# An encoder layer in hi/lo splits: where loads, conversions and the embedding's gate stand in the engines' orders

## The chip, the core and the metric

The kernel runs on one core of a Trainium2 chip. The core has a matrix engine (TensorE, PE in the profile), a vector engine (VectorE, DVE), an engine for activation functions (ScalarE, ACT), a general engine (GpSimd, POOL) and SyncE (SP), which here only issues transfers. Each of them runs its own instructions in order; among each other they are held together by semaphores. Transfers are issued on the queues of SP, ACT and POOL and carried by 16 shared DMA engines. The metric is the device time of one launch, in microseconds. Before the change it was 1231.56 us, the median of three runs (1228.37 to 1232.48).

## The reference

One post-norm encoder layer over 1024 tokens of width 1024, all in float32. Half of the mixer's heads do bidirectional retention, the other half windowed attention; then comes a SwiGLU feed-forward part, and beside it an embedding per layer that a gate lets through.

```python
u = jnp.einsum('bsd,de->bse', h, w_in[i])
rq, rk, rv, rg, aq, ak, av = jnp.split(u, split_points, axis=-1)
y_ret = _bidirectional_retention(rq, rk, rv, lg_f, lg_b, ret_gn_gain[i], rg)   # group norm, times silu(rg)
y_att = _windowed_gqa(aq, ak, av, attn_sink[i])                                # +-128 tokens, ALiBi, sinks
mix = jnp.einsum('bse,ed->bsd', jnp.concatenate([y_ret, y_att], axis=-1), w_out[i])
h = _layer_norm(ALPHA * h + mix, ln1_gain[i], ln1_bias[i])
g = jnp.einsum('bsd,df->bsf', h, w_ffn_gate[i])
up = jnp.einsum('bsd,df->bsf', h, w_ffn_up[i])
ffn = jnp.einsum('bsf,fd->bsd', jax.nn.silu(g) * up, w_ffn_down[i])
ple = jnp.einsum('bsr,rd->bsd', p[i], w_ple_proj[i])
ple_gate = jax.nn.sigmoid(jnp.einsum('bsd,de->bse', h, w_ple_gate[i]))
h = _layer_norm(ALPHA * h + ffn + ple_gate * ple, ln2_gain[i], ln2_bias[i])
```

## The kernel before

Every dense product is made in three matmuls (`mm3`, L82). Each operand is first cut into a high part in the fast matmul type and the rest (`split`, L78): ScalarE copies with rounding (L79), VectorE subtracts (L80). Most dense products also use a seven-product scheme for 2x2 blocks in place of eight, so sums of weight blocks and of activation blocks are made first (POOL and VectorE), and the seven results are added and subtracted behind (VectorE).

The program has five stages, in us of the profiled execution:

- **First products and dense projections**, 0 to about 150. Five pairs of projections, each in seven products. `seq1` (L296) is the order of the products, `x_put(c)` cuts the last sums of activations, `pahead(n)` (L303) cuts the weights of the next products.
- **Mixers**, about 150 to 405, in four head pairs, numbered 0 to 3, with boundaries near 210, 275 and 340. Per pair the retention and the attention are short matmuls with much work of the other engines between. To fill TensorE, a queue of dense work is interleaved: ten tiles of 16 steps (`mtile`, `spill`, `gate`, `embedding`; `enqueue`, L474), 36 steps per pair, taken where the list of `run` (L828 on, built in the loop over the pairs) has an F. Loads and cuts of a tile are hung on the first steps of the tile ahead of it. `load_pair` (L513) loads the next pair's keys, queries and the attention's raw queries, and `conv_q` (L314) converts these for two groups g (ScalarE scales, L323; VectorE takes the rest, L324). `rv_load` and `turned` (L489 to L509) load the retention's values and transpose them on TensorE (L495). `norm` and `scale` are the group norm: VectorE sums, ScalarE squares, POOL takes a power (`sm`, L634), VectorE multiplies (L635). `wsum` (L435) builds sums of the gate's weights in DRAM with POOL transfers (L444 to L448).
- **Output projection and first layer norm**, to 505.
- **Gate products** `ple` (L1058), 505 to 582: h @ w_ple_gate in seven products (`prod`, L1011). Each finished gate tile (128x1024) goes through a sigmoid on ScalarE; `fetch` brings the embedding's product back from DRAM (`ed`), `embed_next` multiplies on VectorE (L1052) and adds to the accumulator `zd` in DRAM by an accumulating transfer (L1053), both transfers on POOL's queue.
- **FFN**: gate and up in 11 weight pairs of 14 products each (`gunits`, 582 to about 1012), down (to 1200), second layer norm (to 1232.6). `Pair.load` brings the weights, `s_sums` makes sums of them on POOL (L1133 to L1139), `prep` cuts, `post` evacuates (L1180, L1186).

What sets the order: in the mixers TensorE and POOL run in the order of the source (`manual_schedule`), while ScalarE, VectorE and SP are ordered by a scheduler at build time. From `ple` on, all engines run in the order of the source. Buffers come from pools; tiles of one tag share a few slots, and a new tile's first writer waits for the old tile's last reader. The tag `raw` (`rawt`, L97) has two slots: raw weights, raw queries and raw values go through them in the mixers.

## Time and profile before

| | us |
|---|---|
| median of three runs | 1231.56 |
| the profiled execution, whole | 1234.39 |
| its span from first to last instruction | 1232.6 |
| TensorE busy | 1201.4 |
| TensorE busy in 150 to 405 (255 us, mixers) | 245.90 |
| TensorE busy in 582 to 1012 (430 us, FFN gate and up) | 421.13 |
| TensorE busy in 1200 to 1232 (32 us, the end) | 23.63 |

The mean granted clock of TensorE was 0.993. A row of a timeline has the start in us, the busy time, the engine, the line of the source, the operation, and out<-in by the names of the program; in square brackets stands the idle time of the engine just before and what ended it. SPq, ACTq and POOLq rows are issues of transfers. A row of the waits names the engine and line that waited, the engine, tile and line it waited for, then the total, the count and the longest. In the rows of windows, PEclk is the clock that TensorE was granted in the stretch, 1.00 being full.

### The profile page before, as it was taken

The numbers are of one execution on the slowest core, as the hardware profiler recorded it, in microseconds if no ns is written. First come the engines' busy times: TensorE is split into PE (matmuls) and PEld (weight loads), VectorE is DVE, ScalarE is ACT, GpSimd is POOL, SyncE is SP. The second block draws the span as 40 slices with busy tenths as digits, with TensorE's granted clock in tenths as the row PEclk, the third lists the DMA queues.
The fourth block names the chain that finished last, engine by engine and source line by source line (L and its number), as shares of the span: only waits on it lengthen the run. The fifth ranks groups of instructions, "written<-read, shape, count | busy, mean of one in ns | idle before, by whom it ended". The sixth has DMA issues, their size and how long they took to land.

```text
span 1232.6 us, 16444 instructions
## 1 busy us (share of the span) xinstructions
PE 1201.4 (97%) x5911; PEld 988.4 (80%) x5911; DVE 760.1 (62%) x1258; ACT 522.8 (42%) x968; POOL 455.7 (37%) x395
## 2 busy tenths in 40 slices
PE   9999999989999999999899999999999999999997
PEld 7778877878887888887688888888888888888885
DVE  6954665666665548884665454555445555875678
ACT  4532555666675502462333223333323334652432
POOL 1651113120111002332477556466564523024235
PEclk9999999999999999999899999999999999999999
DMA  6222445572300432358631233321333149999987
GB/s 222 90 87 103 145 137 150 164 225 92 114 18 18 140 117 96 131 166 241 143 140 74 73 126 128 128 77 69 112 128 128 69 137 281 372 273 209 263 197 204
DMA packets 69521, 178.43 MB, mean 145 GB/s; under 512 B 8128, under 2 KB 10304, under 8 KB 69440
## 3 DMA queue, kind: packets, MB, share of 16 engines
q1 hardware_dynamic: 54016, 139.64, 32.3%
q0 software_dynamic: 14848, 35.66, 14.4%
q10 hardware_dynamic: 576, 2.10, 0.4%
q8 instruction: 46, 0.75, 0.2%
q14 instruction: 35, 0.29, 0.1%
HBM read 124.67 MB, written 47.45 MB: 140 GB/s over the span
## 4 chain that ended last, share of the span: by engine, by line
PE 65%; DMA 13%; DVE 8%; issue 7%; POOL 4%; ACT 3%; ACTq 0%; SPq 0%; DVEq 0%; POOLq 0%
PE bs L287 4%; PE bs L289 4%; PE bs L288 4%; PE bt L287 3%; PE bo L287 3%; PE bt L288 3%; PE bt L289 3%; PE bo L289 3%; PE bo L288 3%; PE bmm L287 3%; PE bmm L288 3%; PE bmm L289 3%; PE bmm L83 3%; PE bmm L85 3%; PE bmm L84 3%
## 5 line engine op out<-in xcount | busy, mean ns | idle before, releaser
L1165 POOL TENSOR_TENSOR ev<-ev 128x512 f32<-128x512 f32 x33 | 54.9, 1663 | 91.0 <-DVE ev L1180 62.2
L80 DVE TENSOR_TENSOR w<-H,w 128x512 fp32r<-128x512 f32 x44 | 42.2, 959 | 65.1 <-ACT w L79 65.1
L80 DVE TENSOR_TENSOR w<-raw,w 128x512 fp32r<-128x512 f32 x55 | 45.8, 841 | 44.9 <-ACT w L79 44.8
L1163 ACT ACTIVATE ev<-ev 128x512 f32<-128x512 f32 x33 | 20.9, 632 | 102.0 <-DVE ev L1180 102.0
L1169 POOL TENSOR_TENSOR ev<-ev,ev 128x512 f32<-128x512 f32 x44 | 62.7, 1436 | 2.6
L83 PE MATMUL bmm<-H,w 128*128 128x512 f32 x144 | 61.3, 426 | 0.3 <-ACT H L79 0.3
L80 DVE TENSOR_TENSOR u<-H,u 128x512 fp32r<-128x512 f32 x47 | 35.5, 755 | 39.4 <-ACT u L79 39.1
L1133 POOL TENSOR_TENSOR H<-ln 128x512 f32<-128x512 f32 x22 | 29.0, 1318 | 81.2 <-DMA ln<-in_w_gu 75.3
L84 PE MATMUL bmm<-H,w 128*128 128x512 f32 x144 | 57.0, 396 | 0.0
L85 PE MATMUL bmm<-H,w 128*128 128x512 f32 x144 | 56.9, 395 | 0.0
L666 POOL COPY sc<-skb 128x2 f32<-128x2 f32 x32 | 6.2, 202 | 135.3 <-PE bt L686 87.6
L852 POOL TENSOR_TENSOR stt<-stt,cst 128x1 f32<-128x1 f32 x8 | 11.5, 1451 | 99.7 <-DVE stt L851 99.7
L79 ACT ACTIVATE u<-H 128x512 fp32r<-128x512 f32 x47 | 29.6, 630 | 40.8 <-PE bmm L289 9.0
L674 ACT ACTIVATE sc<-sc,st 128x385 f32<-128x385 f32 (+1 forms) x64 | 37.3, 584 | 15.9 <-DVE st L671 15.8
L79 ACT ACTIVATE w<-raw 128x512 fp32r<-128x512 f32 x55 | 33.6, 622 | 23.1 <-PE bt L289 6.7
L80 DVE TENSOR_TENSOR u<-raw,u 128x512 fp32r<-128x512 f32 x32 | 36.5, 1146 | 5.8 <-ACT u L79 5.8
L678 ACT ACTIVATE sc<-sc,st 128x384 f32<-128x384 f32 (+1 forms) x64 | 34.1, 580 | 10.4 <-DVE st L676 10.4
L79 ACT ACTIVATE w<-H 128x512 fp32r<-128x512 f32 x44 | 27.4, 622 | 24.4 <-PE bs L289 6.3
L1139 POOL TENSOR_TENSOR H<-H,raw 128x512 f32<-128x512 f32 x22 | 36.8, 1697 | 0.0
L1135 POOL TENSOR_TENSOR H<-H,raw 128x512 f32<-128x512 f32 x22 | 35.0, 1592 | 1.7
L671 DVE CUSTOM_DVE_ANT_0 sc<-cst,bs,skb 128x384 f32<-128x384 f32 (+1 forms) x64 | 35.0, 575 | 0.7 <-PE bs L670 0.4
L83 PEld LDWEIGHTS bmm<-H,w 128*128 128x128 f32 x144 | 27.4, 190 | 6.6 <-issue 1.6
(886 smaller groups left out, 4036.3 us busy)
## 6 DMA issues: line engine op xcount, KB each, us to landing
ad<-ev SPq DMA_DIRECT2D x33, 512.0 KB, 2.6
raw<-in_w_gu SPq DMA_DIRECT2D x22, 512.0 KB, 4.4
ln<-in_w_gu SPq DMA_DIRECT2D x22, 512.0 KB, 3.5
raw<-ad SPq DMA_DIRECT2D x40, 256.0 KB, 5.9
ln<-ad SPq DMA_DIRECT2D x37, 256.0 KB, 6.4
H<-in_w_dn SPq DMA_DIRECT2D x33, 256.0 KB, 7.9
raw<-in_w_mt SPq DMA_DIRECT2D x14, 512.0 KB, 3.6
A<-in_w_pg POOLq DMA_DIRECT2D x12, 512.0 KB, 5.5
```

Of the source, the lines that this page charges most:

```text
L79: act.activation(hi, raw, AF.Copy)
L80: dve.tensor_tensor(lo, raw, hi.bitcast(F32), ALU.subtract)
L83: pe.matmul(o, lh, rh, start=start, stop=False)
L84: pe.matmul(o, lh, rl, start=False, stop=False)
L85: pe.matmul(o, ll, rh, start=False, stop=stop)
L287: pe.matmul(o, lh, rh, start=start, stop=False, skip_group_check=True)
L288: pe.matmul(o, lh, rl, start=False, stop=False, skip_group_check=True)
L289: pe.matmul(o, ll, rh, start=False, stop=stop, skip_group_check=True)
L674: act.activation(sc[:, g, :nk + 1], sc[:, g, :nk + 1], AF.Exp, bias=st_[:, 0, j, g:g + 1], scale=-1.0, accum_out=st_[:, 2, j, g:g + 1])
L1139: pool.tensor_tensor(s[3], s[0], a(0, 1), ALU.subtract)
L1165: pool.tensor_tensor(c[:, 1, :], c[:, 0, :], c[:, 1, :], ALU.mult)
L1169: pool.tensor_tensor(self.ev[dst][:, 0, :], left, right, op)
```

## The change

1. **Dense products.** `pahead(4)` moves ahead of `x_put(3)`, so weights of the first products are cut ahead of the last sums of activations. Product 2 of projection 1 moves from fourth place to between products 7 and 4 of projection 0; in the last projection 2 and 7 change places, and with them the two halves of the attention's queries.
2. **Mixers.** SP, too, now runs in the order of the source. A tile's load stands at step 0 of the tile ahead of it, its two cuts at steps 6 and 9 (step 12 for the embedding's first rows). The cuts are tied on ScalarE behind the activation that the source has just ahead (`in_order`). `load_pair` only loads; the two halves of `conv_q` come later and by themselves (`cq[0]`, `cq[1]`). The embedding fetches its rows two tiles ahead. The steps of `wsum` are spread anew, and the last comes after `M(1)`, the power and scaling of the group norm. The exponentials of the decay matrix `dt` go into one tile, with one POOL product and one sum instead of two each.
3. **Embedding's gate.** `ple` stores each finished gate in DRAM (`gd`, on ScalarE's queue) and fetches, multiplies and accumulates nothing. In the FFN, at products 14, 28 to 112, SP loads one gate and its part of the embedding; at products 21, 35 to 119 VectorE multiplies them and POOL issues the accumulating transfer.

```diff
+    class Scalar:
+        def activation(self, *args, **kw):
+            ins = nc.scalar.activation(*args, **kw)
+            if behind_act[1] and behind_act[0]:
+                tc.add_manual_dep(ins.ins, behind_act[0], mybir.DependencyInfo(
+                    mybir.DependencyClass.NoSync, mybir.DependencyReason.DATA), reason="order")
+            behind_act[0] = ins.ins.name
+            return ins
...
+    def in_order(f):
+        def g(*args):
+            behind_act[1] = True
+            f(*args)
+            behind_act[1] = False
+        return g
...
+    gd = dr.tile([8, P, 2, HF], F32, name="gd")
...
-    seq1 = [(0, 1), (1, 1), (0, 2), (1, 2)]
-    for n in range(len(projs)):
-        seq1 += [(n, 6), (n, 5)] + ([(n, 2)] if n > 1 else []) + [(n, 7)]
-        seq1 += ([(n + 1, 1)] if 0 < n < len(projs) - 1 else []) + [(n, 4), (n, 3)]
+    seq1 = [(0, 1), (1, 1), (0, 2), (0, 6), (0, 5), (0, 7), (1, 2), (0, 4), (0, 3)]
+    for n in range(1, NPJ - 1):
+        seq1 += [(n, 6), (n, 5)] + ([(n, 2)] if n > 1 else []) + [(n, 7), (n + 1, 1), (n, 4), (n, 3)]
+    seq1 += [(NPJ - 1, p) for p in (6, 5, 7, 2, 4, 3)]
...
+        pahead(4)
         x_put(3)
-        pahead(4)
...
-                for k, f in enumerate(tiles[n + 1][0]):
-                    steps[2 * k] = lambda f=f, g=steps[2 * k]: both(f, g)
+                for k, f in zip((0, 6, 9, 12), tiles[n + 1][0]):
+                    steps[k] = lambda f=f if k == 0 else in_order(f), g=steps[k]: both(f, g)
...
-        pairs.append((rk, rq, conv_q(i, r)))
+        qs = [kt_("q", 3) for _ in range(2)]
+        pairs.append((rk, rq, qs))
+        return lambda g: in_order(conv_q)(i, r, qs, None, (g,))
...
-    with tc.manual_schedule(engines={ET.PE, ET.Pool}):
+    with tc.manual_schedule(engines={ET.PE, ET.Pool, ET.SP}):
...
-            more = ((lambda: load_pair(i + 1),), (lambda: hold.update(t=rv_load(i + 1)),)) if i < 3 else ((lambda: None,),) * 2
+            more = ((lambda: hold.update(q=load_pair(i + 1)),), (lambda: hold.update(t=rv_load(i + 1)),)) if i < 3 else ((lambda: None,),) * 2
+            cq = [(lambda g=g: hold["q"](g),) if i < 3 else (lambda: None,) for g in range(2)]
...
-                val(3), Q(1), more[0], F, trn(4), sco(6), ws[4], F, val(4), Y(1, 0), F, trn(5), sco(7), more[1], ws[5], F,
-                val(5), Y(1, 1), N(1), F, trn(6), ws[6], F, nt[0], nt[1], val(6), M(1), F, trn(7), F], 36)
+                val(3), Q(1), more[0], F, trn(4), sco(6), F, val(4), Y(1, 0), ws[4], F, trn(5), sco(7), more[1], cq[0], F,
+                val(5), Y(1, 1), N(1), ws[5], F, trn(6), cq[1], F, nt[0], nt[1], val(6), M(1), F, trn(7), ws[6], F], 36)
...
+    def keep_gate(t, h, g):
+        act.dma_start(gd[EMB.index((t, h))], g)
+
+    def embed_load(n):
+        parts[n] = ct([P, 2, HF], "pe", 1), ct([P, 2, HF], "sg", 1)
+        sp.dma_start(parts[n][0], gd[n])
+        sp.dma_start(parts[n][1], rows(ed, *EMB[n]))
+
+    def embed(n):
+        g, e = parts[n]
+        dve.tensor_tensor(g, g, e, ALU.mult)
+        pool.dma_start(rows(zd, *EMB[n]), g, accum_op=ALU.add)
...
                     act.activation(r[4 + k // 2], r[4 + k // 2], AF.Sigmoid, scale=sc_)
-                    embed(t + k - 1, h, r[4 + k // 2])
+                    keep_gate(t + k - 1, h, r[4 + k // 2])
...
-            if k == 0:
-                embed_next()
+            if k % 14 == 0 and 0 < k < 14 * 9:
+                embed_load(k // 14 - 1)
+            if k % 14 == 7 and 14 < k < 14 * 9:
+                embed(k // 14 - 1)
```

Three places show how the instructions stand now. The first is VectorE at the end of pair 2, around the group norm of its second half. `q` is the converted query of pair 3 for one group, `raw` its raw rows, `sm` and `ym` are the group norm's sums and values, `ptr` a copy of transposed scores, `qq` a product for the retention. Before:

```order
L324 SCALAR_TENSOR_TENSOR q_2967<-raw_2964,q_2967 64x1024
L676 RECIPROCAL st_2831<-st_2831 128x2
L590 TENSOR_TENSOR qq_3223<-rkq_2961,qd_3178 128x512
L622 TENSOR_REDUCE sm_3096<-bo_3034 128x8
L590 TENSOR_TENSOR qq_3223<-rkq_2961,qd_3178 128x512
L624 SCALAR_TENSOR_TENSOR ym_3098<-sm_3096,bo_3034 128x512
L691 COPY ptr_3114<-bt_3110 128x384
L628 TENSOR_REDUCE sm_3096<-sq_3100 128x8
L629 TENSOR_SCALAR sm_3096<-sm_3096 128x8
L635 TENSOR_TENSOR ym_3098<-ym_3098,sm_3096 128x512
```

And with the change:

```order
L620 TENSOR_TENSOR qq_3212<-rkq_2953,qd_3170 128x512
L652 TENSOR_REDUCE sm_3080<-bo_3016 128x8
L354 SCALAR_TENSOR_TENSOR q_2958<-raw_2956,q_2958 64x1024
L654 SCALAR_TENSOR_TENSOR ym_3082<-sm_3080,bo_3016 128x512
L721 COPY ptr_3098<-bt_3094 128x384
L620 TENSOR_TENSOR qq_3212<-rkq_2953,qd_3170 128x512
L658 TENSOR_REDUCE sm_3080<-sq_3084 128x8
L659 TENSOR_SCALAR sm_3080<-sm_3080 128x8
L354 SCALAR_TENSOR_TENSOR q_2959<-raw_2956,q_2959 64x1024
L107 TENSOR_TENSOR w_3108<-raw_3003,w_3108 128x512
L665 TENSOR_TENSOR ym_3082<-ym_3082,sm_3080 128x512
```

Before, the first group's conversion lay some forty rows ahead and the second (`q_2967`) stood ahead of the group norm's sums. Now both stand among the group norm's steps, and the second (`q_2959`) is behind its last sum.

The second place is SP, the issues of the loads for pair 3 in the mixers. `rkq` are the retention's keys and queries, `raw<-ud 128x1024` is either the attention's raw queries (L518 before, L546 now) or the retention's values (L509 before, L537 now), `raw<-in_w_mt` the weights of a tile in the queue, `pr<-in_pT` and `ed<-es` the embedding's rows and results. Before:

```order
L518 DMA raw_2964<-ud 128x1024
L757 DMA ed<-es_2706 128x512
L757 DMA ed<-es_2744 128x512
L734 DMA pr_2804<-in_pT 128x256
L111 DMA raw_3015<-in_w_mt 128x1024
L734 DMA pr_2847<-in_pT 128x256
L757 DMA ed<-es_2786 128x512
L734 DMA pr_2884<-in_pT 128x256
L757 DMA ed<-es_2816 128x512
L734 DMA pr_2928<-in_pT 128x256
L509 DMA raw_3076<-ud 128x1024
```

And with the change:

```order
L543 DMA rkq_2952<-ud 128x1024
L544 DMA rkq_2953<-ud 128x1024
L546 DMA raw_2956<-ud 128x1024
L797 DMA ed<-es_2963 128x512
L797 DMA ed<-es_3000 128x512
L141 DMA raw_3003<-in_w_mt 128x1024
L537 DMA raw_3058<-ud 128x1024
L141 DMA raw_3263<-in_w_mt 128x1024
L141 DMA raw_3535<-in_w_mt 128x1024
```

Before, the raw queries (`raw_2964`) were loaded well ahead and the values (`raw_3076`) took the slot of the weights `raw_3015`. Now the three loads of `load_pair` stand together, then a tile's weights, then the values; `raw_3058` takes the slot of `raw_2956` and so waits for the last reader of that, VectorE's `q_2959` above.

The third place is POOL between the end of the gate products and the FFN's first sums of weights (`H`). `zd<-A` is the accumulating transfer, `pe<-ed` and `sg<-ed` are fetches of the embedding, `ln` and `raw` hold the FFN's weights; L1043 and L1044 of the changed kernel are sums of activations for the gate products. Before:

```order
L1053 DMA zd<-A_4526 128x2x512
L1043 DMA pe_5084<-ed 128x2x512
L1053 DMA zd<-A_4527 128x2x512
L1043 DMA sg_5115<-ed 128x2x512
L1133 TENSOR_TENSOR H_4520<-ln_5049 128x512
L1135 TENSOR_TENSOR H_4520<-H_4520,raw_5047 128x512
L1133 TENSOR_TENSOR H_4520<-ln_5067 128x512
L1135 TENSOR_TENSOR H_4520<-H_4520,raw_5065 128x512
L1053 DMA zd<-A_4764 128x2x512
L1053 DMA zd<-A_4765 128x2x512
L1137 TENSOR_TENSOR H_4520<-ln_5049,raw_5047 128x512
L1137 TENSOR_TENSOR H_4520<-ln_5067,raw_5065 128x512
```

And with the change:

```order
L1043 TENSOR_TENSOR ln_4627<-h_4142,ln_4627 128x512
L1044 TENSOR_TENSOR ln_4627<-ln_4627,h_4142 128x512
L1167 TENSOR_TENSOR H_4509<-ln_5022 128x512
L1169 TENSOR_TENSOR H_4509<-H_4509,raw_5020 128x512
L1167 TENSOR_TENSOR H_4509<-ln_5041 128x512
L1169 TENSOR_TENSOR H_4509<-H_4509,raw_5039 128x512
L1171 TENSOR_TENSOR H_4509<-ln_5022,raw_5020 128x512
L1171 TENSOR_TENSOR H_4509<-ln_5041,raw_5039 128x512
L1173 TENSOR_TENSOR H_4509<-H_4509,raw_5020 128x512
L1173 TENSOR_TENSOR H_4509<-H_4509,raw_5039 128x512
```

All transfers are gone from here. The eight accumulating ones stand in the FFN now, one in each of eight weight pairs.

More of the change, by code (lines that the diff above doesn't have):

```diff
@@ L98, in rawt, with unit2_parts, load, cut @@
         return wp.tile([P, w], F32, tag="raw", bufs=2, name=nm("raw"))
-    def unit(src, pl=None, tag="w", cut=1):
-        r = rawt(HF)
-        sp.dma_start(r, src)
-        t = (pl or wp).tile([P, 2, HF], F32R, tag=tag, bufs=4, name=nm("w"))
-        split(r, t[:, 0, :], t[:, 1, :])
-        return t
-    def unit2(src, pl=None, tag="w"):
-        r = rawt(2 * HF)
-        sp.dma_start(r, src)
-        ts = []
-        for i in range(2):
+    def unit2(src, pl=None, tag="w"):
+        load, ts = unit2_parts(src, pl, tag)
+        load()
+        for f in ts[1]:
+            f()
+        return ts[0]
+    def unit2_parts(src, pl=None, tag="w"):
+        hold, ts = {}, []
+        def load():
+            hold["r"] = rawt(2 * HF)
+            sp.dma_start(hold["r"], src)
+        def cut(i):
             t = (pl or wp).tile([P, 2, HF], F32R, tag=tag, bufs=4, name=nm("w"))
-            split(r[:, i * HF:(i + 1) * HF], t[:, 0, :], t[:, 1, :])
+            split(hold["r"][:, i * HF:(i + 1) * HF], t[:, 0, :], t[:, 1, :])
             ts.append(t)
-        return ts
+        return load, (ts, [lambda: cut(0), lambda: cut(1)])
     def big16(shape=(P, 2, 2, S)):
@@ L312, in slope, with conv_q @@
         return 2.0 ** -(i + 4 * g + 1)
-    def conv_q(i, raw, qs=None, cs=None):
-        if qs is None:
-            qs = [kt_("q", 3) for _ in range(2)]
+    def conv_q(i, raw, qs, cs=None, gs=(0, 1)):
         for c in cs or [slice(0, S)]:
-            for g in range(2):
+            for g in gs:
                 sc_ = 0.125 / slope(i, g)
@@ L414, in layer @@
             if pr is projs[-1]:
-                {6: lambda: keys(hs[0]), 5: lambda: keys(hs[1]), 2: lambda: queries(hs[0]),
-                 7: lambda: queries(hs[1])}.get(p, lambda: None)()
+                {6: lambda: keys(hs[0]), 5: lambda: keys(hs[1]), 7: lambda: queries(hs[0]),
+                 2: lambda: queries(hs[1])}.get(p, lambda: None)()
             pahead(k + 1 + min(5, 4 + k))
@@ L457, in mtile @@
         hold = {}
-        def load():
-            hold["w"] = unit2(w_mt[idx])
+        load, (ws_, cuts) = unit2_parts(w_mt[idx])
         def step(h, kt):
@@ L464, in step @@
                 hold["b"] = bank("mm")
-            b, w = hold["b"], hold["w"][kt // 4]
+            b, w = hold["b"], ws_[kt // 4]
             c = slice((kt % 4) * P, (kt % 4 + 1) * P)
@@ L470, in step @@
                 evac(b, h)
-        return [load], [lambda h=h, kt=kt: step(h, kt) for h in range(2) for kt in range(KT)]
+        return [load] + cuts, [lambda h=h, kt=kt: step(h, kt) for h in range(2) for kt in range(KT)]
     def enqueue(tiles):
@@ L730, in embedding, with fetch, cut @@
         wpe, ps = [], {}
+        prs = {}
+        def fetch(t):
+            if t < NT:
+                prs[t] = bt([P, 2 * P], "pr", 2)
+                sp.dma_start(prs[t], pT[t])
         def prep(t):
-            r = bt([P, 2 * P], "pr", 2)
-            sp.dma_start(r, pT[t])
-            ps[t] = bt([P, 2, 2 * P], "p", 2, F32R)
-            split(r, ps[t][:, 0, :], ps[t][:, 1, :])
+            if t < NT:
+                ps[t] = bt([P, 2, 2 * P], "p", 2, F32R)
+                split(prs[t], ps[t][:, 0, :], ps[t][:, 1, :])
+        raw = {}
         def load():
-            prep(0)
-            r = rawt(2 * HF)
-            sp.dma_start(r, w_pe[h])
-            for q in range(2):
-                wpe.append(atile((P, 2, HF), F32R))
-                split(r[:, hs[q]], wpe[q][:, 0, :], wpe[q][:, 1, :])
+            raw["r"] = rawt(2 * HF)
+            sp.dma_start(raw["r"], w_pe[h])
+            fetch(0)
+            fetch(1)
+        def cut(q):
+            wpe.append(atile((P, 2, HF), F32R))
+            split(raw["r"][:, hs[q]], wpe[q][:, 0, :], wpe[q][:, 1, :])
         def step(t, q):
             if q == 0:
-                if t + 1 < NT:
-                    prep(t + 1)
+                fetch(t + 2)
+                in_order(prep)(t + 1)
                 hold["b"] = bank("mm")
@@ L757, in step @@
                 sp.dma_start(ed[t][:, hs[h]], e)
-        return [load], [lambda t=t, q=q: step(t, q) for t in range(NT) for q in range(2)]
+        return [load, lambda: cut(0), lambda: cut(1), lambda: prep(0)], [lambda t=t, q=q: step(t, q) for t in range(NT) for q in range(2)]
     def run(steps, total):
@@ L1031, in quad @@
         return [ts[k // 2][:, k % 2, :] for k in range(4)] + ts
[L1033 removed]
+    EMB = [(0, 0), (2, 0), (4, 1), (6, 1), (0, 1), (2, 1), (4, 0), (6, 0)]
+    parts = {}
     def rows(x, t, h):
         return x[t:t + 2, :, hs[h]].rearrange("t p c -> p t c")
[L1038 to L1056 removed]
+    def keep_gate(t, h, g):
[8 more added lines that the diff above has]
+        pool.dma_start(rows(zd, *EMB[n]), g, accum_op=ALU.add)
     def ple(ahead):
@@ L1082, in c00 @@
             if k % 2:
-                embed(k - 1, 0, g[4 + k // 2])
+                keep_gate(k - 1, 0, g[4 + k // 2])
         L = lambda f, *ts: [lambda t=t: f(t) for t in ts]
-        E = [embed_next]
         b1 = banks(MS)
```

53 lines of the change are left out of this document (20 added, 33 removed).

## The prediction

> **What bounds the kernel now.** I read the page's busy times first, then TensorE's waits, then stretches of a fixed length with the granted clock.
>
> ```profile
> PE 1201.4 (97%) x5911; PEld 988.4 (80%) x5911; DVE 760.1 (62%) x1258; ACT 522.8 (42%) x968; POOL 455.7 (37%) x395
> ```
>
> TensorE is the bound: 31.2 of 1232.6 us are left beside it, and no other engine is above 62%. The change leaves TensorE's instructions as they are in number and size, and moves 52 of them in the first stage. So it can only win or lose idle time of TensorE, and clock. The waits, longest in total first (engine, line waiting, what it waited for, total us, times, longest):
>
> ```profile
> PE bmm L287 <- ACT ev L1186: 4.4, 1, 4.4
> PE bmm L289 <- DVE u L80: 3.8, 1, 3.8
> PE bo L701 <- DVE ptr L691: 2.5, 1, 2.5
> ...
> PE bt L495 <- ACT ptr L689: 1.6, 1, 1.6
> ```
>
> Each is a single stall, so each has one place and can be costed alone. The first two lie between the gate products and the FFN. What the place costs is seen from matmuls per 50 us, where 688 to 738 is the FFN running full (after the length: busy us and instructions of PE, PEld, DVE, ACT and POOL, then granted clock, DMA share, GB/s):
>
> ```profile
> 550.00:600.00 50.00, 41.76 (x171) 33.41 (x170) 29.63 (x39) 14.71 (x23) 19.26 (x18) 0.94 0.81 200
> 600.00:650.00 50.00, 49.37 (x216) 40.53 (x216) 30.37 (x35) 16.86 (x28) 31.02 (x23) 0.99 0.48 142
> 688.00:738.00 50.00, 50.00 (x222) 41.42 (x221) 26.30 (x34) 15.61 (x27) 30.32 (x21) 1.00 0.22 79
> ```
>
> At the full pace 444 matmuls fit into 550 to 650 and 387 ran. 57 missing at 50/222 = 0.225 us are 12.8 us: 8.2 in the two stalls, 0.6 idle in 600 to 650 (50 less 49.37), and 4.0 that the lowered clock took after them, about 2 us for each long stall.
>
> **Gates kept in DRAM (-12.3).** Why the FFN starts late, from the engines' timelines (start, duration, engine; in brackets the idle time before and what ended it):
>
> ```profile
> 576.04 1.22 POOL L1053 DMA_DIRECT2D zd<-A  x1 [7.44 <-issue]
> ...
> 578.46 1.23 DVE L1052 TENSOR_TENSOR A<-A,pe 128x1024 f32<-128x1024 f32 x1 [7.05 <-DMA pe<-ed]
> 584.62 1.22 DVE L1052 TENSOR_TENSOR A<-A,sg 128x1024 f32<-128x1024 f32 x1 [3.73 <-DMA sg<-ed]
> ...
> 591.99 1.40 POOL L1133 TENSOR_TENSOR H<-ln 128x512 f32<-128x512 f32 x1
> ...
> 586.50 0.50 PE L289 MATMUL bmm<-h,u 128*128 128x512 f32 x1 [3.81 <-DVE u L80]
> 597.83 0.80 PE L287 MATMUL bmm<-h,u 128*128 128x512 f32 x1 [4.42 <-ACT ev L1186]
> ```
>
> VectorE runs in order. It holds the embedding multiplication until the fetched embedding has landed, and behind it stand the last product's additions and the splits of the FFN's operands. POOL has the same fetches and the accumulating stores ahead of the FFN's weight sums, so the first sum starts at 591.99, after the FFN's first matmuls (586.50). The changed kernel puts none of this here. What stays is a store of each finished gate, issued on ScalarE's queue. Such an issue on a hardware queue took 0.33 us (the row from 309.41 below), so eight cost ScalarE 2.6 us over some 50, where it is busy 14.71 of 50. I take 12.3 of the 12.8 and leave 0.5 for a first operand that is a little late. Bounds: the whole 12.8, and 0 if another wait stands at the same place.
>
> The removed work comes back in the FFN eight times, once in each of eight groups of 14 FFN products (38 us a group):
>
> ```profile
> 722.44 1.29 POOL L1133 TENSOR_TENSOR H<-ln 128x512 f32<-128x512 f32 x1 [8.57 <-DMA ln<-in_w_gu]
> ...
> DMA to landing us min/median/max: 4.8/5.7/10.5
> ...
> 712.00:750.00 38.00, 38.00 (x169) 31.49 (x168) 19.65 (x25) 11.83 (x20) 22.25 (x16) 1.00 0.28 103
> ```
>
> One multiplication (1.23 at 578.46) and the issue of one accumulating store on POOL (1.22 at 576.04) come to a stretch in which VectorE has 18.4 and POOL 15.8 us free. The two loads go out half a group, some 19 us, ahead of the multiplication, and `pe`'s fetches landed within 10.5 us even at a DMA share of 0.81; here it is 0.28. POOL's second half of the weight sums moves back by up to 5 us. The sums are used in the next group, so the cover is over 10 us. I cost it at 0; were the cover gone, each group would stall by the one multiplication and the issue, 8 x 2.4 = 19 us.
>
> **Dense products reordered (-2.5).**
>
> ```profile
> 58.82 0.50 PE L289 MATMUL bs<-H,w 128*128 128x512 f32 x1 [1.63 <-DVE w L80]
> 73.14 0.47 PE L287 MATMUL bo<-T,u 128*128 128x512 f32 x1 [0.87 <-DVE A L270]
> ```
>
> In the first stall the split of a weight operand stood on ScalarE and VectorE behind the splits of the last activations; it now stands ahead of them. Ahead of the product that waited in the second, another one has been put that needs nothing fresh. A stall of this size costs no clock (the row pair at 208 to 214 below). Bounds 0 and -2.5.
>
> **Mixers, start of pair 0 and boundary to pair 1 (-2.0 and -1.6).** Rows of ScalarE, then of TensorE:
>
> ```profile
> 160.95 1.06 ACT L323 ACTIVATE q<-raw 64x1024 fp32r<-64x1024 f32 x1 [3.28 <-DMA raw<-ud]
> ...
> 208.14 0.63 ACT L79 ACTIVATE A<-raw 128x512 fp32r<-128x512 f32 x1 [4.10 <-DMA raw<-in_w_pe]
> ...
> 162.54 0.44 PE L549 MATMUL bt<-cst,A 128*128 128x128 f32 x2 [0.73 <-ACT v L496]
> 163.83 0.44 PE L669 MATMUL bs<-k,q 128*128 128x384 f32 x1 [0.85 <-DVE st L671]
> 166.14 1.16 PE L559 MATMUL bt<-rv,kdec 128*128 128x128 f32 x8 [0.58 <-DVE kdec L551]
> ```
>
> ScalarE runs in order too. At 160.95 and 208.14 it had been blocked by a conversion whose load had not landed, and TensorE paid 0.73 + 0.85 + 0.58 = 2.2 and 1.6 us soon after. Now loads go out at a tile's first step and cuts follow six and nine steps later, so neither blocks. I take 2.0 (bounds 1.5 and 2.5) and 1.6 (0 and 1.6).
>
> **Mixers, boundary from pair 1 to pair 2 (-5.2).** Timeline rows, then windows with the clock, of this place and of the boundary before it:
>
> ```profile
> 272.73 0.55 POOL L444 DMA_DIRECT2D ws<-A  x1 [6.31 <-DMA A<-in_w_pg]
> 273.29 1.69 POOL L634 TENSOR_TENSOR sm<-sm,cst 128x8 f32<-128x8 f32 x1
> ...
> 276.89 0.69 PE L701 MATMUL bo<-ptr,v 128*64 128x128 f32 x2 [2.45 <-DVE ptr L691]
> ...
> 276.00:278.00 2.00, 0.83 (x4) 0.43 (x6) 0.83 (x2) 1.16 (x4) 1.11 (x2) 0.64 0.00 0
> 278.00:282.00 4.00, 4.00 (x26) 3.34 (x28) 2.16 (x3) 2.50 (x5) 2.00 (x4) 0.50 0.19 70
> 282.00:284.00 2.00, 2.00 (x13) 1.54 (x10) 1.29 (x2) 0.00 (x0) 0.00 (x0) 0.65 0.00 0
> ...
> 208.00:210.00 2.00, 0.37 (x4) 0.28 (x4) 1.20 (x2) 1.86 (x4) 0.00 (x0) 1.00 0.65 262
> 210.00:214.00 4.00, 4.00 (x31) 3.17 (x30) 2.18 (x5) 2.23 (x6) 3.54 (x4) 1.00 0.67 197
> ```
>
> POOL held the group norm's power (L634) behind the store of a weight sum that waited 6.31 for its load; VectorE's scaling and a score copy queued up behind that. After the idle the clock fell: (1 - 0.50) x 4 + (1 - 0.65) x 2 = 2.7 us, with 0.3 before it 3.0. The smaller stall at 209 left the clock at 1.00. The change puts the power ahead of the last store, so 2.45 + 0.28 (the second gap of that row's group) + 3.0 = 5.7 go. Left over I count 0.5, since the embedding's second weight load is issued only when a transposition has let its buffer go. Bounds -1 and -5.7.
>
> [...]
>
> **A new stall, boundary from pair 2 to pair 3 (+9).** SP now issues in the order of the source, and two buffers (`raw`) serve the queries' raw rows, the tiles' weights and the values' raw rows in turn. Of pair 3 the values' load takes the buffer of its queries' raw rows, whose second half is now converted on ScalarE and VectorE just one block ahead of the transpositions (L495) that read the values. Before (timeline rows of SP, ScalarE, VectorE and TensorE, then two landing times of 290 to 345):
>
> ```profile
> 309.41 0.33 SPq L509 DMA_DIRECT2D raw<-ud  x1
> ...
> 330.10 0.91 ACT L678 ACTIVATE sc<-sc,st 128x256 f32<-128x256 f32 x2 [0.36 <-DVE st L676]
> ...
> 328.65 1.22 DVE L324 SCALAR_TENSOR_TENSOR q<-raw,q 64x1024 fp32r<-64x1024 f32 x1 [0.47 <-ACT q L323]
> ...
> 331.34 0.68 DVE L622 TENSOR_REDUCE sm<-bo 128x8 f32<-128x512 f32 x1
> ...
> 334.25 1.04 PE L495 MATMUL bt<-cst,raw 128*128 128x128 f32 x8
> ...
> raw<-ud SPq DMA_DIRECT2D x2, 512.0 KB, 4.1
> ...
> rkq<-ud SPq DMA_DIRECT2D x1, 512.0 KB, 3.1
> ```
>
> The load went out 24.8 us early. Now, on the same clock and with these durations: ScalarE scales the first half after the exponentials, 331.0 to 332.1 (1.06, the row from 160.95); VectorE, after the reduction, cuts it to 333.3, centres the output (0.6) to 333.9; ScalarE squares that (0.6) to 334.5 and scales the second half to 335.6; VectorE, after a copy, a product, the next reduction and a small step (0.5 + 0.6 + 0.7 + 0.2), cuts the second half from 335.8 to 337.0. SP issues there, and 3.1 to 4.1 us later the data is in, 340.1 to 341.1. The transpositions were due at 334.25, and TensorE runs in order, so everything behind them waits: 5.9 to 6.9, I take 6.4. On SP the weights of the next tile stand behind this load, but they are needed only after 16 more steps of the queue. The clock loss behind it was 2 and 3 us in the two places above: 2.5. Together 9. Bounds: 0 (the conversion comes earlier than VectorE's order has it), 11 (6.9 + 3.0, and 1 for what queues up).
>
> At the two earlier boundaries the values take a buffer whose last cut lies five blocks back, so they are in time. The embedding's rows, two tiles ahead, may hold ScalarE now and then behind 1.5 MB of the pair's loads: +0.8, bounds 0 and 2. One larger POOL product in place of two, the eleven ScalarE instructions less and the other shifts hide under TensorE: 0; the most they can bring is what is idle there now, under 1 us.
>
> **Sum.** -12.3 - 2.5 - 2.0 - 1.6 - 5.2 + 9.0 + 0.8 = -13.8. The profiled execution took 1234.4 (span 1232.6 and 1.8 around it), so 1220.6; the median shown is 2.8 below that execution, so **1218**.
>
> **Rivals.** *No late values* (0.22): everything else holds, but the second cut does not stand in the way of the load, because VectorE or SP gets to it sooner. For it: the load was early by 24.8 us, a large margin. Against: the order shows the cut as the last reader of that buffer. 1218 - 9 = 1209. *The FFN still starts late* (0.12): gates out of the buffers only when stored, weight loads behind the stores at a DMA share of 0.81; the embedding goes but the stall stays, whole or half: 1218 + 6 to 12 = 1224 to 1230. Against it: the stores replace fetches of the same size, and nothing on VectorE waits for them. *Slower* (0.08): SP in source order blocks on a buffer at all three boundaries of pairs, as I expect it at one. It decides from the point at which a values' load goes out less than 3.6 us (a landing) ahead of its transpositions. Two more stalls of 9 make 1236. Against it are the five blocks at the other two boundaries.
>
> **How the numbers follow.** The forecast has 0.58, with 1213 to 1223 as its own range. Of 1231.6, 0.3% is 3.7 us, about what a measurement can tell: faster means under 1227.9. All of the forecast and of the first rival count as faster, and half of the second (0.05, rounded down): 0.85. The other 0.07 is no change, 0.08 slower. The range 1207 to 1228 leaves out the slower case, the second rival's upper half, and some 0.05 below 1207.
>
> **What would show it.** Right: no idle of TensorE above 1 us between 550 and 640; no idle at the earlier boundaries; at the end of pair 2 one idle of 6 to 7 us ended by the DMA of `raw` from `ud`, the issue of which comes right after VectorE's second `q` cut; FFN groups of 38.0 us. Wrong: that load issued before the second cut (then 1209); FFN groups above 38.2 (the added work isn't hidden); the first FFN matmuls still waiting for `u` or `ev`; or waits for `pr` on ScalarE that reach TensorE.

## The result, and the profile after

The changed kernel took 1223.06 us (median of five runs, 1221.77 to 1224.99) against 1231.55 of the kernel before: a ratio of 0.9936, 95% interval 0.9918 to 0.9953. Measured again beside other kernels on another chip it was 1222.16 against 1232.26, 0.9914 (0.9899 to 0.9929). The forecast was 1218 with a range of 1207 to 1228; its own, narrower range of 1213 to 1223 is missed by a hair. The profiled execution of the changed kernel took 1221.87 us, 12.5 less than that of before; the forecast for this execution had been 1220.6. The profiled execution of before lay 2.8 us above its median, this one 1.2 below its own, so the profiles flatter the change: by the medians the gain is 8.5 us, and 10.1 on the other chip, where 13.6 had been forecast. What follows compares the traces.

First the waits of TensorE, the whole top of the list (engine, line that waited, what it waited for, total us, times, longest):

```profile
PE bt L523 <- DMA raw<-ud: 6.0, 1, 6.0
PE bmm L110 <- ACT p L51: 5.6, 6, 3.3
PE bo L383 <- POOL s L380: 1.3, 1, 1.3
PE bs L699 <- DVE pt L617: 0.8, 2, 0.6
PE bt L318 <- DVE A L1113: 0.7, 1, 0.7
```

Every stall that the forecast had read from the kernel before is gone or under 1 us (of the one at the boundary to pair 2, 0.5 is left). Two new waits stand in their place, both in the mixers: the values' load, which the forecast had at 6.4 us, and waits for the embedding's rows, for which it had left 0.8 in all. (All activations now carry the line of the wrapper, L51; `p` is the embedding's cut rows.)

The FFN, in windows over the stage and over its steady part (after the length: busy us and instructions of PE, PEld, DVE, ACT and POOL, granted clock, DMA share, GB/s):

```profile
582.00:1012.00 430.00, 430.00 (x1899) 356.18 (x1898) 241.98 (x293) 135.18 (x229) 247.45 (x170) 1.00 0.43 137
...
712.00:750.00 38.00, 38.00 (x170) 31.46 (x169) 22.14 (x26) 11.69 (x21) 23.27 (x17) 1.00 0.45 143
```

TensorE is busy for all 430 us, where it was for 421.13. In a steady group VectorE went from 19.65 to 22.14 us and POOL from 22.25 to 23.27, and the pace stayed at 38 us.

Because TensorE runs the same matmuls in nearly the same order in both kernels, the start of one and the same matmul in the two traces tells how far ahead the changed kernel is at that place. From one place to the next this is the ledger of the change:

| between, on the clock of before | what lies there | forecast, us | shift in the traces, us |
|---|---|---|---|
| 12 to 152 | dense products | -2.5 | -2.7 |
| 152 to 170 | start of pair 0 | -2.0 | -3.2 |
| 205 to 218 | boundary to pair 1 | -1.6 | -2.6 |
| 230 to 265 | embedding's first half, rows | +0.8 | +5.9 |
| 265 to 290 | boundary to pair 2 | -5.2 | -5.4 |
| 290 to 333 | embedding's second half | in the 0.8 above | +0.6 |
| 333 to 342 | boundary to pair 3, values' load | +9.0 | +8.4 |
| 342 to 580 | output projection, gate products | 0 | +0.5 |
| 580 to 640 | start of the FFN | -12.3 | -13.0 |
| 640 to 1190 | FFN | 0 | -0.1 |
| 1190 to 1212 | second norm | 0 | -1.4 |
| sum | | -13.8 | -13.0 |

(Unrounded, the matmul at 1212 starts 12.95 us earlier.)

### The profile page after: what moved, and what is told of

It reads as the page before. It is cut to its first block, busy times and chain, and to the rows that moved or that the text cites. A ratio compares the mean times of both kernels' runs of the same rounds, so it can differ in the third digit from the quotient of the medians.

```text
span 1219.7 us, 16421 instructions
## 1 busy us (share of the span) xinstructions
PE 1195.1 (98%) x5911; PEld 985.5 (81%) x5911; DVE 764.3 (63%) x1258; ACT 525.3 (43%) x968; POOL 448.5 (37%) x379
## 3 DMA queue, kind: packets, MB, share of 16 engines
q0 software_dynamic: 13696, 31.46, 13.6%
## 4 chain that ended last, share of the span: by engine, by line
PE 90%; DVE 5%; DMA 2%; POOL 1%; issue 1%; ACT 1%; DVEq 0%; SPq 0%; POOLq 0%; ACTq 0%
PE bs L318 5%; PE bs L320 5%; PE bs L319 5%; PE bmm L320 5%; PE bmm L318 5%; PE bmm L319 5%; PE bt L318 5%; PE bt L320 5%; PE bt L319 5%; PE bo L320 5%; PE bo L318 5%; PE bo L319 5%; PE bmm L110 4%; PE bmm L112 4%; PE bmm L111 4%; PE bo L731 2%
## 5 line engine op out<-in xcount | busy, mean ns | idle before, releaser
L51 ACT ACTIVATE sc<-sc,st 128x385 f32<-128x385 f32 (+3 forms) x128 | 71.3, 582 | 27.0 <-DVE st L701 17.8
L1167 POOL TENSOR_TENSOR H<-ln 128x512 f32<-128x512 f32 x22 | 33.0, 1500 | 126.0 <-DMA ln<-in_w_gu 126.0
L1199 POOL TENSOR_TENSOR ev<-ev 128x512 f32<-128x512 f32 x33 | 52.1, 1579 | 56.5 <-DMA h<-in_w_dn 24.1
L107 DVE TENSOR_TENSOR u<-H,u 128x512 fp32r<-128x512 f32 x47 | 45.4, 967 | 40.3 <-ACT u L51 40.2
L1203 POOL TENSOR_TENSOR ev<-ev,ev 128x512 f32<-128x512 f32 x44 | 67.3, 1539 | 2.6
L51 ACT ACTIVATE ev<-ev 128x512 f32<-128x512 f32 x33 | 20.9, 632 | 107.0 <-DVE ev L1214 107.0
L51 ACT ACTIVATE w<-raw 128x512 fp32r<-128x512 f32 x72 | 43.6, 622 | 25.9 <-PE bo L112 6.2
L51 ACT ACTIVATE u<-H 128x512 fp32r<-128x512 f32 x47 | 29.5, 628 | 38.9 <-POOL H L1169 8.8
L51 ACT ACTIVATE u<-raw 128x512 fp32r<-128x512 f32 x43 | 26.2, 629 | 29.6 <-PE bt L320 8.0
L51 ACT ACTIVATE w<-H 128x512 fp32r<-128x512 f32 x44 | 27.4, 622 | 23.3 <-PE bmm L320 6.6
L1171 POOL TENSOR_TENSOR H<-ln,raw 128x512 f32<-128x512 f32 x22 | 34.3, 1562 | 0.0
L1169 POOL TENSOR_TENSOR H<-H,raw 128x512 f32<-128x512 f32 x22 | 32.1, 1461 | 1.7
L1314 POOL DMA_DIRECT2D h<-in_w_dn x24 | 21.3, 899 | 31.2 <-issue 16.6
```

The source lines that it names most:

```text
L51: ins = nc.scalar.activation(*args, **kw)
L107: dve.tensor_tensor(lo, raw, hi.bitcast(F32), ALU.subtract)
L1171: pool.tensor_tensor(s[2], a(1, 0), a(0, 0), ALU.subtract)
L1199: pool.tensor_tensor(c[:, 1, :], c[:, 0, :], c[:, 1, :], ALU.mult)
L1203: pool.tensor_tensor(self.ev[dst][:, 0, :], left, right, op)
```

## The experiments

Runs e1 to e4 shared one chip and its runs of the kernel before (1235.14 us), e5 to e8 another (1232.26), e9 to e11 a third (1233.39). Ratios are to the kernel before on the same chip; shifts in a trace are read as in the table. "The changed kernel" is the one of this document.

### The values' load: e1

In the changed kernel, SP, VectorE and TensorE at the boundary to pair 3 show these rows:

```profile
329.72 0.32 SPq L537 DMA_DIRECT2D raw<-ud  x1
...
324.64 1.22 DVE L354 SCALAR_TENSOR_TENSOR q<-raw,q 64x1024 fp32r<-64x1024 f32 x1
328.48 1.22 DVE L354 SCALAR_TENSOR_TENSOR q<-raw,q 64x1024 fp32r<-64x1024 f32 x1
...
332.95 1.94 PE L523 MATMUL bt<-cst,raw 128*128 128x128 f32 x8 [5.96 <-DMA raw<-ud]
```

The second cut ends at 329.70, SP issues at 329.72, the data is in 3.2 us later. On the clock of before (7.4 us more) the issue is at 337.1, where the forecast had 337.0. That the cut causes it is tested by moving it one block forward:

```diff
- ... val(4), Y(1, 0), ws[4], F, trn(5), sco(7), more[1], cq[0], F,
- ... trn(6), cq[1], F, nt[0], ...
+ ... val(4), Y(1, 0), ws[4], cq[0], cq[1], F, trn(5), sco(7), more[1], F,
+ ... trn(6), F, nt[0], ...
```

> The changed kernel, with both halves of the next pair's queries converted behind Y(1, 0), one block before the values' load, instead of at cq[0] and cq[1] after it. Theory: the values' load waits for that conversion alone. It goes out some 9 us earlier, the one stall of 5.96 us (PE bt L523 <- DMA raw<-ud) and the clock lost behind it go, 8.0 us in all by the shift between the two traces there: 1215. The two waits for the embedding's rows stay. Rival: the load is late for another reason (SP's queue or the transfer itself), the stall stays: 1223. Second rival: it goes, but another wait takes its place within the next blocks: 1219 to 1223.

Measured: 1212.75, ratio 0.9834 (0.9816 to 0.9852). Rows of its SP and VectorE:

```profile
321.52 0.32 SPq L537 DMA_DIRECT2D raw<-ud  x1
...
320.28 1.22 DVE L354 SCALAR_TENSOR_TENSOR q<-raw,q 64x1024 fp32r<-64x1024 f32 x1 [0.48 <-ACT q L51]
```

Again the issue follows the cut at once, now 8 us earlier, and the transpositions find their data: the stall is gone from the list of waits. Against the trace of the changed kernel, this place alone gained 8.4 us (6.1 at the transpositions and 2.3 in the 5 us behind them, the clock). The theory held; neither rival did. (Elsewhere this execution lost 1.5 us: the long wait for rows, 3.1 us here, was followed by half the clock, which that of 3.3 in the changed kernel was not. The last section has both kinds.)

### The embedding's rows: e2

The largest of the six waits, in the changed kernel's SP, ScalarE and TensorE:

```profile
249.60 0.32 SPq L797 DMA_DIRECT2D ed<-es  x1
250.03 0.45 SPq L767 DMA_DIRECT2D pr<-in_pT  x1
...
257.26 0.42 ACT L51 ACTIVATE p<-pr 128x256 fp32r<-128x256 f32 x1 [3.50 <-DMA pr<-in_pT]
...
257.73 0.50 PE L110 MATMUL bmm<-A,p 128*128 128x512 f32 x1 [3.32 <-ACT p L51]
```

In the source's order a row's fetch stands on SP behind the store of an earlier tile's result, which waits for TensorE and ScalarE. So the fetch keeps pace with TensorE and cannot run ahead. This one landed 7.2 us after its issue, behind 1.5 MB of pair 2's loads (issued from 245.01 to 247.04).

```diff
-                prs[t] = bt([P, 2 * P], "pr", 2)
+                prs[t] = bt([P, 2 * P], "pr", 3)
-            fetch(0)
-            fetch(1)
+            for t in range(3):
+                fetch(t)
-                fetch(t + 2)
+                fetch(t + 3)
```

> The changed kernel, with the embedding's rows fetched three tiles ahead into three buffers instead of two ahead into two. Theory: TensorE's 5.6 us of waits at L110 <- p come from rows fetched only when the store of the tile before has been issued, with 2 to 4 us between fetch and use; one tile more of lead removes them all: 1217.5. The stall of 5.96 us stays. Rival: the largest of them, 3.3 us, comes from the pair's 1.5 MB ahead on the DMA engines, and a row fetched behind these is late all the same: only some 2 us go, 1221.

Measured: 1216.65, ratio 0.9857 (0.9840 to 0.9874). Its waits:

```profile
PE bt L523 <- DMA raw<-ud: 6.1, 1, 6.1
PE bo L383 <- POOL s L380: 1.3, 1, 1.3
PE bmm L110 <- ACT p L51: 1.1, 3, 0.7
```

From 5.6 to 1.1 us of waits, and 4.7 us in the shift of the traces there. One tile more of lead is enough even for the fetch behind the pair's loads, so the rival's larger wait went as well: behind the pair's loads, with the DMA engines at a share of 1.00 (252.55 to 255.97), the landing took 7.2 us where the median of the changed kernel's 16 fetches is 3.3, and the short lead made a stall of it.

### Both together, and only where it is needed: e3, e6, e9

> Both edits together: conversion of the queries one block earlier, rows three tiles ahead. Theory: the two losses stand at different places and add up, 8.0 + 5.5: 1209.5. Rival: they share a cause (SP's order), or one only hides the other: 1215 or above.

Measured: 1208.39, ratio 0.9788 (0.9773 to 0.9803). In the trace e3 is 12.5 us ahead of the changed kernel at 342, of which 2.1 belong to the first 12 us of this execution (see the last section). That leaves 10.4 of the 13.1 that the two edits gained apart (8.4 and 4.7): the theory's sum falls short by 2.7. A new stall took it. ScalarE, then TensorE, in e3:

```profile
252.61 1.06 ACT L51 ACTIVATE q<-raw 64x1024 fp32r<-64x1024 f32 x1 [2.35 <-DMA raw<-ud]
...
255.56 0.88 PE L731 MATMUL bo<-ptr,v 128*64 128x128 f32 x12 [2.40 <-DVE ptr L721]
```

With the rows no longer holding TensorE, the early conversion of pair 2's queries comes before their load has landed (issued at 243.24, used at 252.61). ScalarE stands still, and the copy of the scores with it: 2.4 us, and behind it the clock is at 0.50 from 258 to 260 (3.8 us in all by the shift). So e6 leaves the conversion early for pair 3 alone:

```diff
+            ce, cl = (cq, [none] * 2) if i == 2 else ([none] * 2, cq)
- ... ws[4], cq[0], cq[1], F, trn(5), sco(7), more[1], F,
+ ... ws[4], ce[0], ce[1], F, trn(5), sco(7), more[1], cl[0], F,
- ... trn(6), F, nt[0], ...
+ ... trn(6), cl[1], F, nt[0], ...
```

> Rows three tiles ahead, and the queries converted early only ahead of pair 3; ahead of pairs 1 and 2 the conversions stand as in the changed kernel. Theory: with both edits everywhere, the 2.4 us stall at 255.6 arose since the raw queries of pair 2 landed only at 252.6 and ScalarE waited 2.35 us for them; put back there, that stall and the clock behind it (3.8 us in the shift of the traces) go, all else stays: 3.8 below both edits together, about 14 us or 1.15% better than the changed kernel on the same chip less 3 to 4 more, so 17 in all. Rival: the stall is due to the rows' transfers crowding the pair's loads, and stays or moves: no better than both edits together (13 to 14 us below the changed kernel).

Measured: 1206.69, 15.5 us less than the changed kernel beside it (e5), ratio 0.9788 (0.9771 to 0.9805). No stall above 1.3 us is left in its trace:

```profile
PE bo L383 <- POOL s L380: 1.3, 1, 1.3
PE bmm L110 <- ACT p L51: 1.1, 3, 0.7
PE bs L699 <- DVE pt L617: 0.8, 2, 0.6
```

In this trace the place went as the theory had it: between 230 and 265 (on the clock of before) this kernel loses 0.75 us against the kernel before, where e3 loses 3.2, and between 333 and 342 it loses nothing. The rival falls, too: pair 2's raw queries take 8.2 us to land here, 9.3 in e3 and 9.3 in the changed kernel, whose rows run two tiles ahead, so the rows don't crowd them. The ratio is that of e3, though, within the intervals; on time alone the two aren't told apart. Repeated on a third chip:

> Rows three tiles ahead and the early conversion ahead of pair 3 only, once more, as a measure on the chip of the two runs beside it: 0.979 of the kernel before.

Measured: 1208.84, ratio 0.9804 (0.9784 to 0.9824). In this second execution the 2.4 us stall is gone as well, but one row came late again (1.3 us; its waits for `p` are 2.3 in all, and 2.7 us are lost between 230 and 265). At 337, the start taken off, the two executions are 3.6 and 1.6 us ahead of e3. So three tiles of lead are not always enough, and what the later conversion ahead of pair 2 saves is settled only to within these 2 us.

This version beats both kernels: the changed one by 1.3% (e6 beside e5), the one before by 2.0 to 2.1%.

### What the mixers' part was worth: e4, e5

e4 is the kernel before, with the new order of the dense products and the gates in DRAM; the mixers and SP's order are left as they were.

```diff
-        x_put(3)
         pahead(4)
+        x_put(3)
...
+    gd = dr.tile([8, P, 2, HF], F32, name="gd")
...
-                    embed(t + k - 1, h, r[4 + k // 2])
+                    keep_gate(t + k - 1, h, r[4 + k // 2])
```

> The kernel before, with the dense products' order and the gates in DRAM of the changed kernel, and the mixers left as they were. Theory, by the shift between the two traces: the mixers' part went from 2.5 us ahead (at 150) to 0.5 behind (at 400), so it costs 3.0 net, and without it the time is 1220. By the terms of the prediction it would cost 1.0 net: 1222. Rival: the mixers' part is what brought the gain, and the gates little: 1228 or above.

Measured: 1221.63, ratio 0.9889 (0.9873 to 0.9906), against 0.9914 (0.9899 to 0.9929) for the changed kernel when it was run again:

> The changed kernel once more, as a measure on the chip of the three runs beside it: 0.993 to 0.994 of the kernel before, as measured first, with the stall of 6 us at pair 2 to 3 and 5 to 6 us of waits for rows.

(That run came out a little better than expected: 0.9914 for 0.993 to 0.994, with the stall at 6.2 us and 4.4 us of waits for rows.) By time the two aren't told apart: e4's ratio is lower by 0.0025, some 3 us, but the intervals overlap. By the traces they are the same: 12.75 us ahead of the kernel before at 1212 on its clock, against 12.95 for the changed kernel. But they get there differently, and here my reading of the ledger failed. I had taken the dense products' 2.8 us as kept. ScalarE and TensorE of e4, then windows behind its first two gaps:

```profile
154.50 1.06 ACT L325 ACTIVATE q<-raw 64x1024 fp32r<-64x1024 f32 x1 [3.96 <-DMA raw<-ud]
...
156.09 0.44 PE L551 MATMUL bt<-cst,A 128*128 128x128 f32 x2 [2.55 <-ACT rv L498]
...
156.60:160.00 3.40, 3.40 (x13) 2.83 (x12) 1.57 (x4) 0.81 (x3) 0.00 (x0) 0.50 0.72 265
...
207.80:211.20 3.40, 3.40 (x19) 2.54 (x20) 1.58 (x4) 2.51 (x6) 2.67 (x3) 0.50 0.64 177
```

The stage ends 3.0 us earlier. At 170 the lead is 2.0, after the boundary to pair 1 it is 1.05, after that to pair 2 it is 0.2. Most of this is not longer waiting. At the start of pair 0 ScalarE does wait longer for its load, 3.96 for 3.28 us, and the scheduler has put this conversion ahead of copies (`rv`, `v`) that TensorE needs; but TensorE's idle is 2.55 us against 2.5 (0.33 + 0.73 + 0.85 + 0.58). It stands in one piece here, and half the clock follows it, which it did not behind the four small gaps (1.00 from 162 to 175 in the kernel before). At the boundary to pair 1 the gap is 1.6 us in both, and again the clock falls behind it in e4 alone (the kernel before has 1.00 there, the rows of 208 to 214 in the prediction). Only at the boundary to pair 2 is the wait longer, 3.1 for 2.5. The two drops of the clock are 3.4 us at half, 1.7 us each by these rows, and a gap of 1.6 us was followed by one in this execution and not in that of the kernel before. So that the mixers as before take the earlier start back is not shown. From 152 to 342 e4 loses 2.8 us to the kernel before; the changed kernel wins 11.2 there (3.2 + 2.6 + 5.4) and loses 14.9 (5.9 + 0.6 + 8.4), 3.8 in all with what is rounded away. So in these traces the mixers' part as it stands came out about 1 us worse than the mixers left alone. The theory's 3.0 is neither borne out nor refuted: without the two drops e4 would stand further ahead, and the medians have it 3 us ahead, within their uncertainty.

The gates in DRAM are what the whole gain of the change comes to: in e4, which has nothing of the mixers' part, the shift from 580 to 640 is -13.0 as well.

### The work moved into the FFN: e7

```diff
-                embed_load(k // 14 - 1)
+                pass
...
-                embed(k // 14 - 1)
+                pass
```

> The changed kernel without the embedding in the FFN: the two loads, the multiplication and the accumulating transfer of each of the eight groups are left out, so the gated embedding is missing from the output. Theory: they are hidden by 18 us of free time of VectorE and 16 of POOL per group, so nothing changes: within 2 us of the changed kernel on the same chip. Rival: they cost up to 2.4 us per group, 19 us in all.

Measured: 1221.64, beside 1222.16 of the changed kernel on the same chip; both 0.9914. The windows of the stage, of e7 and then of e5:

```profile
640.00:1000.00 360.00, 360.00 (x1590) 298.20 (x1589) 184.21 (x234) 110.63 (x187) 200.64 (x135) 1.00 0.28 103
```

```profile
640.00:1000.00 360.00, 360.00 (x1590) 298.20 (x1589) 200.46 (x247) 109.90 (x187) 208.53 (x142) 1.00 0.43 137
```

16 us of VectorE, 8 of POOL and a third more DMA traffic (137 for 103 GB/s) leave 1590 matmuls in 360 us as they were. Matmul by matmul the two traces stay 5.13 us apart from 580 to 640 and to 1000. The cover that the forecast had named (18 and 16 us per group) is real, and the term of 0 is shown.

### The ties behind ScalarE's work: e8, e10

```diff
-            behind_act[1] = True
+            behind_act[1] = False
```

> The changed kernel without the ties behind ScalarE's work; loads, steps and SP's order stay. The scheduler then puts the cuts and conversions earlier on ScalarE. Theory: they come ahead of their loads' landing and block ScalarE, as in the kernel before at 160.95 and 208.14, so 4 to 6 us at the start of pair 0 and at its end come back; but the second half of pair 3's queries is cut earlier as well, so the values' stall of 8 us goes: -4 to +2 against the changed kernel. Rival: the ties did nothing that the later steps don't do alone: -8, the values' stall gone and nothing back.

Measured: 1213.64, 8.5 us below the changed kernel beside it, ratio 0.9845 (0.9824 to 0.9865). ScalarE's rows that ended a wait for a load, in pairs 0 and 1:

```profile
181.06 1.06 ACT L51 ACTIVATE q<-raw 64x1024 fp32r<-64x1024 f32 x1 [1.08 <-DMA raw<-ud]
...
230.65 0.63 ACT L51 ACTIVATE w<-raw 128x512 fp32r<-128x512 f32 x1 [2.14 <-DMA raw<-in_w_mt]
```

The theory's mechanism is there, cuts that come ahead of their load, but these waits are shorter than the slack of TensorE, and the starts of pair 0 and pair 1 stay as in the changed kernel (6.2 us ahead at 170, 8.2 at 218, the start taken off). So the tie is not what had cured these places. The later steps of loads and cuts and SP's new order remain; no run separates the two. Ahead of pair 3 the second cut comes at 318.53, the values' load goes out at 319.78, and the stall is gone. So the rival held: the ties bought nothing and held the late conversion in its place.

> The changed kernel without the ties behind ScalarE's work, and with the rows three tiles ahead; the conversions stay where the change put them. Theory: the ties have no use once loads and steps are where they are, their only effect is the late conversion ahead of pair 3: the same time as with the early conversion (within 2 us), as the scheduler does that by itself. Rival: without ties some cut stands ahead of its landing on ScalarE and costs a stall: 2 to 5 us above.

Measured: 1207.28, beside 1208.84 of e9; ratios 0.9794 (0.9775 to 0.9814) and 0.9804 (0.9784 to 0.9824), the same. The profiled execution is 3.8 us below that of e9, but 1.9 of these lie in the first 12 us. The theory held: with rows three tiles ahead and no ties, the scheduler finds the early conversion by itself (the second cut starts at 314.74, the values' load goes out at 315.99).

### The order of the dense products, in the best version: e11

```diff
-    seq1 = [(0, 1), (1, 1), (0, 2), (0, 6), (0, 5), (0, 7), (1, 2), (0, 4), (0, 3)]
+    seq1 = [(0, 1), (1, 1), (0, 2), (1, 2)]
...
-        pahead(4)
         x_put(3)
+        pahead(4)
```

> Rows three tiles ahead and the early conversion ahead of pair 3, with the dense products in the order of the kernel before. Theory, by the trace of the changed kernel: the first stage's 2.5 us come back and nothing behind absorbs them: 2.5 above e9. Rival, by the run with the mixers as before, where the first stage's gain was gone by 158 us: the start of the mixers waits for something that doesn't depend on the products' order, and the time is within 1 us of e9.

Measured: 1212.06, ratio 0.9825 (0.9805 to 0.9846); beside it e9 with 0.9804 (0.9784 to 0.9824). The intervals overlap: 3.2 us between the medians, about 2.5 of uncertainty on each. Its waits have the stalls of the kernel before again:

```profile
PE bs L320 <- DVE w L107: 1.6, 1, 1.6
...
PE bo L318 <- DVE A L301: 0.9, 1, 0.9
```

In the traces it is 2.8 us behind e9 at 152 (0.5 of start taken off), 1.2 after the embedding's first half, and 0.7 from 300 to 1000, where e9's late row has taken some of it; behind e6, the same kernel as e9, it is some 2.7 at 1000. Something between 0.7 and 3 us is what the order is worth in this version; it isn't settled closer.

## Why the prediction was right, step by step

**Gates in DRAM, -12.3.** Shown, at -13.0 in the changed kernel and in e4. No operand was late at all, so the 0.5 us left over for that wasn't needed. Of the 4.0 us that the forecast put down to the clock, the rows show 3.4: two stretches of 3.4 us at half, from 587.18 and 597.42. The rival of an FFN that still starts late fell: TensorE is busy for 430.00 of 430 us from 582 to 1012.

**The work in the FFN, 0.** Shown by e7, to a tenth of a microsecond in the trace.

**Dense products, -2.5.** -2.7 where they stand. The trace of e4 has lost them again by pair 2, mostly to the clock; e11 leaves 0.7 to 3 us for them. That a stall of this size costs no clock is no rule: it held at 1.63 and 0.87 us here, and e4 paid for one of 1.6.

**Start of pair 0 and boundary to pair 1, -2.0 and -1.6.** -3.2 and -2.6, both in the forecast's direction and a good half larger. The forecast had counted the named stalls alone. At the boundary 1.9 us go at the stall, and 0.6 in waits of 0.15 to 0.3 us each behind it. The cause, loads and cuts standing elsewhere, fits what the traces show; e8 shows that the ties had no share, and whether the later steps or SP's order did it stays open.

**Boundary to pair 2, -5.2.** -5.4, 3.1 of it the clock: from 276.57 to 283.40 the kernel before had 6.23 us of TensorE's work at half.

**The values' load, +9.** +8.4, with the idle 5.96 for 6.4. The chain of the forecast, from scaling by ScalarE to SP's issue, came out to 0.1 us on the same clock, and e1 shows that it is the cause. The rival without this stall fell for the changed kernel; it describes e6, which was measured at 15.5 us below the changed kernel, about half of that from this place.

**The embedding's rows, +0.8.** This is the term that was mis-sized: +5.9 in the first half and +0.6 in the second. (The same mixers lost 6.1 in the first half in e5 and 8.7 in e7, where the long wait was 3.9 us and half the clock followed.) The forecast had named waits for `pr` that reach TensorE as a sign of being wrong, and this sign came. The forecast's sentence was that the rows "may hold ScalarE now and then behind 1.5 MB of the pair's loads". That happened once (3.3 us). The rest, 2.3 us in five waits, comes from what the forecast didn't see: a fetch on SP stands behind the store of a result of TensorE, so two tiles of lead are in fact the time of two short steps. The upper bound of 2 had been set by ScalarE's block alone, without asking what stands ahead of the fetch on its queue.

**The second norm, 0.** -1.4: the stall of 1.2 us at 1208 in the kernel before (VectorE's accumulation) isn't in the trace after. e2 has one of 1.0 there and e4 has none. Nothing was tried on it, so its cause stays open.

The sum was -13.8 against -13.0 in the traces. Two errors met in it: 6 us too little for the rows, and 5 us too little gained over the other places. That they nearly cancel is luck. The clock was right in size where the forecast used it: 2.5 for the values' stall, and half the clock over the 4.9 us from 332.95 to 337.9 is 2.5.

## What to carry to other kernels

When a queue is put into the order of the source, ask of each issue what stands ahead of it there: a prefetch behind a store waits for the engine whose result is stored, and its lead in tiles is worth only as much time as these tiles take (here the fetch went out 0.43 us after the store, and TensorE waited up to 3.32 us). When a conversion is moved later, look for what takes its buffer next: the buffer's next load moves with it, and the transfer's whole landing time is added at the first reader (here 3.2 us, in a stall of 5.96). When a gain seems to be lost again further on, compare idle time and granted clock apart: here the idle was nearly the same (2.55 us in e4 and 2.5 in the kernel before), and the clock behind it was not (0.50 and 1.00).
